# A gated pooling and neighbourhood-attention layer on one core: gate products and operand differences moved to GpSimd, attention's gate taken out of its operand set, heads packed evenly

## The chip, the cores and the metric

One core of a Trainium2 chip runs the whole layer as one program. The metric is the device time of one execution in microseconds (us), the median over the runs shown. Engines are called TensorE (PE in the profile; PEld is its weight load), VectorE (DVE), ScalarE (ACT), GpSimd (POOL) and SyncE (SP). Each works through its own queue in order.

## The reference, cut to what matters

There are 512 + 256 tokens of 2048 features, all in float32.

```python
ada = jax.nn.silu(c) @ w_ada + b_ada
shift, scl, gate = jnp.split(ada, 3, axis=-1)
h = _rms(x, norm_g) * (1 + scl[:, None, :]) + shift[:, None, :]
proj = h @ w_in
...
pool_u, pool_z, q, k, v, attn_z, g_pool, g_attn = jnp.split(proj, cuts, axis=-1)
pool_y = _pool_mixer(pool_u, pool_w, pool_scale) * jax.nn.silu(pool_z)
...
attn_y = _neighbourhood_attention(q, k, v, rpb) * jax.nn.silu(attn_z)
merged = jax.nn.sigmoid(g_pool) * (pool_y @ w_pool_up) + jax.nn.sigmoid(g_attn) * (attn_y @ w_attn_up)
return x + gate[:, None, :] * (merged @ w_o)
```

`proj` has 80 tiles of 128 features: 8 each of pool_u, pool_z, q, k, v and attn_z, 16 of g_pool and 16 of g_attn.

## The kernel before, in words

Activations lie with features on the 128 partitions and all 768 tokens along the free dimension, in tiles of 128x768 float32 (two halves of 384). A "slot" of the `slab` pool holds one such tile; there are 45 (`SLOTS`, L44), and the builder counts what is live.

**Products.** Each float32 number is cut into a high part (a cast to float32r) and a low part (the rest), and a product is three matmuls: high by high, high by low, low by high. A matmul has 128x128 weights and 384 columns. Two output features are made together by `pair_job` (L345), a scheme with seven products (`PRODUCTS`, L47) in place of eight: it needs sums of weights (`add`, L351) and differences of operands. So an operand `Set` (L187) holds, for each of four pairs of feature tiles, four raw quarters (B11, B12, B21, B22) and four differences (T1 to T4), each a slot with a high and a low half. `put` (L191) makes one: ScalarE casts the high part (L194), and VectorE subtracts for the low part (L198), which is held back in `behind` until the next put (`flush`, L181). `differences` (L215) makes T1 to T4 in place, on VectorE (L218, L222, L223, L230), each right before its put. `build` (L237) lists the tasks of a set: load two tiles, optionally work on them (`make`), put four quarters, then four differences. The weights go through `split_next` (L320): cast on ScalarE (L329), subtraction on VectorE (L330), three products ahead of use.

**Stages.** XA and XB are the two halves of `h` (1024 features each) against `w_in`; XA's results are stored as partial sums (`part_d`), XB's are added to them by an accumulating DMA. XR is the pooled branch against `w_pu`, XY the attention branch against `w_au`, MA and MB are the two halves of `merged` against `w_o`. Each of the last four stages (`eight`, L968) has an opening of two features by plain products (16 steps), and seven pair jobs of 14 steps. A step is six matmuls. The opening reads all four pairs' raw quarters within its 16 steps, the differences follow from the 17th step on.

**Order of the work.** The program is written out by a planner. `steps` (L423) yields once a step; `tick` (L168) then runs what was planned for this step (`at`, `after`) and `pump` (L158), which takes the first task of the list if its condition holds, if there is room in the slots (tasks' need plus `heap["spare"]`) and if the pace allows: every third step among pair products, every second where the set is being used up (`drop`), every step among plain products. It also takes `chores`, spaced by their own numbers. If a product needs an operand that is not there, `need` (L284) takes tasks at once until it is (`hurry`). The engines' waits follow from the data.

**Around the change.** XB ends with 32 pair jobs of which eight heads' q, k, v are part. `attention` (L549) plans the six units of a head, 7 or 8 steps apart, by `at`; the first five heads (`DENSE`, L862) begin 42 steps apart, the last three 56, with one or two gate jobs between. When attention's steps have been run (`run(done)`, L1191), XR's set and then XY's are built (L1196, L1197), 31 steps before XB's last step. XY's set loads the attention output and its gate feature (`attended`, L1171), takes Silu of it on ScalarE and multiplies on VectorE (`gated`, L1176): four tiles a pair. The results of XR and XY pass `pu_done` (L904) and `au_done` (L914): a sigmoid of a stored gate tile on ScalarE (`sig_take`, L900) when the result is ready, a product on VectorE, then a store, or an accumulating add and a store. `x_make` (L1135) scales and modulates XB's tiles on VectorE.

```python
def need(st, op, j):
    hurry["on"] = True
    while (op, j) not in st.ops:
        assert tasks and room() >= tasks[0][0] and tasks[0][1](), (st.name, op, j, heap, len(tasks))
        tasks.pop(0)[2]()
```

Of the kernel before, what the change touches and what calls it, by code (L numbers as in the profile page):

```python
# [43 lines left out]
SLOTS = 45  # L44
# [7 lines left out]
def encoder_layer(ctx: ExitStack, tc: tile.TileContext, xT, cT, w_ada2, w_ada4, b_ada, norm_g, w_in, pool_w,  # L52
# [134 lines left out]
    class Set:  # L187
# [3 lines left out]
        def put(self, op, j, src, then=None):  # L191

            t = self.ops[op, j] = slot(f"{self.name}{op}", F32R)
            act.copy(t[:, 0, :], src)  # L194
            flush()

            def rest():
                dve.tensor_tensor(t[:, 1, :], src, t[:, 0, :].bitcast(F32), op=ALU.subtract)  # L198
                if then is not None:
                    then()  # L200

            behind["fn"] = rest
            behind["of"] = t
# [10 lines left out]

    def differences(st, j, a, b):  # L215

        def t1():
            dve.tensor_tensor(a[:, 0, :], a[:, 0, :], a[:, 1, :], op=ALU.subtract)  # L218
            st.put("T1", j, a[:, 0, :])

        def t2():
            dve.tensor_tensor(a[:, 1, :], b[:, 1, :], a[:, 1, :], op=ALU.subtract)  # L222
            dve.scalar_tensor_tensor(b[:, 1, :], a[:, 0, :], -1.0, b[:, 1, :], op0=ALU.mult, op1=ALU.subtract)  # L223
            st.put("T2", j, b[:, 1, :])

        def t3():
            st.put("T3", j, a[:, 1, :], free)

        def t4():
            dve.scalar_tensor_tensor(b[:, 0, :], b[:, 1, :], -1.0, b[:, 0, :], op0=ALU.mult, op1=ALU.subtract)  # L230
            st.put("T4", j, b[:, 0, :], free)

        return t1, t2, t3, t4
# [3 lines left out]
    def build(st, load, ready=lambda j: True, make=None, more=0, whole=0):  # L237


        got = [{} for _ in range(st.pairs)]  # L240

        def fetch(j):
            got[j]["a"], got[j]["b"] = load(j)
            got[j]["t"] = clock["now"]

        def put(j, op):
            k, h = RAW[op]
            st.put(op, j, got[j][k][:, h, :])

        def diff(j, n):  # L250
            g = got[j]
            if n == 0:
                g["d"] = differences(st, j, g["a"], g["b"])
            g["d"][n]()

        def fetches(j):
            tasks.append((2 + more, lambda: ready(j), lambda: fetch(j)))

        def puts(j):
            here = lambda: clock["now"] >= got[j]["t"] + 5 or hurry["on"]  # L260
            if make is not None:
                for k in "ab":
                    tasks.append((0, here, lambda k=k: make(j, k, got[j][k])))
            for op in RAW:
                tasks.append((1, here, lambda op=op: put(j, op)))

        for j in range(whole):
            fetches(j)
            puts(j)
            for n in range(4):  # L270
                tasks.append((1, lambda: True, lambda j=j, n=n: diff(j, n)))
        if whole < st.pairs:
            fetches(whole)
        for j in range(whole, st.pairs):
            if j + 1 < st.pairs:
                fetches(j + 1)
            puts(j)
        for n in range(4):
            for j in range(whole, st.pairs):
                tasks.append((1, lambda: True, lambda j=j, n=n: diff(j, n)))  # L280
# [581 lines left out]
    DENSE = 5  # L862
# [32 lines left out]
    def sig_load(f):  # L895
        state["sig", f] = slot("sig")
        sp.dma_start(flat(state["sig", f]), part_d[G0 + f])

    def sig_take(f):
        t = state["sig", f]  # L900
        act.activation(flat(t), flat(t), AF.Sigmoid)  # L901
        return t

    def pu_done(f):  # L904
        def go(i, t):
            sg = sig_take(f)
            dve.tensor_tensor(flat(t), flat(t), flat(sg), op=ALU.mult)
            pool.dma_start(mp_d[f], flat(t))
            free()
            release(t, 3)  # L910
            sig_load(f + 2)
        return go

    def au_done(f):  # L914
        def go(i, t):
            sg = sig_take(16 + f)
            dve.tensor_tensor(flat(t), flat(t), flat(sg), op=ALU.mult)  # L917
            free()
            if 16 + f + 2 < 32:
                sig_load(16 + f + 2)  # L920

            def add():
                pool.dma_start(flat(t), mp_d[f], accum_op=ALU.add)
                after(5, out)
# [5 lines left out]
            add()  # L930
# [74 lines left out]
    with tc.tile_pool(name="start", bufs=1, reuse_waits="tile") as sp_:  # L1005
# [44 lines left out]
        def modulate(g):  # L1050
# [14 lines left out]
            after(4, rest_)  # L1065
# [69 lines left out]
        def x_make(j, k, t):  # L1135
            dve.tensor_tensor(flat(t), flat(t), flat(rstd), op=ALU.mult)
            apply(8 + 2 * j + (k == "b"), t)
# [33 lines left out]
    def attended(j):  # L1171
        got = stored(attn_d, 2 * j)
        state["az", j] = stored(part_d, AZ0 + 2 * j)
        return got

    def gated(j, k, t):  # L1176
        z = state["az", j][k == "b"]
        act.activation(flat(z), flat(z), AF.Silu)
        dve.tensor_tensor(flat(t), flat(t), flat(z), op=ALU.mult)
        free()  # L1180

    with tc.tile_pool(name="attn", bufs=1, reuse_waits="tile") as at_:
# [7 lines left out]
        done = first - 56 + 40 + 16 - now  # L1190
# [6 lines left out]
    build(XY, attended, lambda j: True, gated, 2, 1)  # L1197
    run(31 * 14 - done)
    for f in range(2):
        sig_load(f)  # L1200
    run(16 + 7 * 14)
# [94 lines left out]
```

## Time and profile before

| | |
|---|---|
| three runs, us | 2041.11, 2044.99, 2046.67 |
| median, us | 2044.99 |
| the profiled execution, us | 2051.03 |
| its span from first to last instruction, us | 2049.3 |
| TensorE busy in the span | 1939.6 us (95%) |
| VectorE, ScalarE, GpSimd busy | 1330.4 us (65%), 1023.1 us (50%), 259.8 us (13%) |
| mean granted TensorE clock, full speed = 1 | 0.973 |

Matmuls are pipelined, so a busy TensorE is not one at its peak; the count of matmuls in a stretch tells more. Idle time of the other engines costs nothing by itself. A wait is put down to what released it last.

### The profile page before, as it was taken

What the parts mean: (1) busy time and instruction counts of PE and PEld (TensorE: products, weight loads), DVE (VectorE), ACT (ScalarE), POOL (GpSimd) and SP (SyncE); (2) the same over time, 40 slices, a digit from 0 to 9 for tenths busy, and PEclk for the clock granted to TensorE, in tenths of its full rate; (3) what the DMA queues carried; (4) which work ended last, traced back from release to release, by engine and by line L of the source; (5) the groups of instructions that cost most, each with busy time, mean ns of one, the idle gap of its engine ahead of it and who ended that gap; (6) DMA issues with size and microseconds to landing.
All of it is one profiled execution on the core that took longest, in us unless ns stands there. A gap on an engine that the chain in (4) does not pass through costs nothing. (4 is left out here: it accounts for less than half of the span.)

```text
span 2049.3 us, 31584 instructions
## 1 busy us (share of the span) xinstructions
PE 1939.6 (95%) x11812; PEld 1832.7 (89%) x11812; DVE 1330.4 (65%) x2392; ACT 1023.1 (50%) x2207; POOL 259.8 (13%) x385
## 2 busy tenths in 40 slices
PE   3999999999999989999999999999989979999998
PEld 2889888898999979999998999999979968999997
DVE  5755555555667777866666667667667767776654
ACT  4433333333344444545656566565556555556553
POOL 0000000000000045410000010010100001112111
PEclk9999999999999999999999999999989989999999
DMA  9755555554343425554544344554556556867765
GB/s 355 248 197 188 190 191 191 201 192 157 117 150 138 162 57 143 135 132 106 119 106 122 93 110 122 109 121 123 132 164 216 214 158 180 243 180 191 211 172 144
DMA packets 100361, 331.92 MB, mean 162 GB/s; under 512 B 13168, under 2 KB 18288, under 8 KB 100208
## 3 DMA queue, kind: packets, MB, share of 16 engines
q1 hardware_dynamic: 68256, 217.35, 31.5%
q0 software_dynamic: 30944, 112.48, 23.8%
q8 instruction: 92, 1.51, 0.3%
q14 instruction: 61, 0.50, 0.1%
q10 hardware_dynamic: 1008, 0.09, 0.0%
HBM read 251.22 MB, written 78.64 MB: 161 GB/s over the span
## 5 line engine op out<-in xcount | busy, mean ns | idle before, releaser
L330 DVE TENSOR_TENSOR wlo<-wraw,whi 128x512 fp32r<-128x512 f32 (+1 forms) x357 | 247.2, 693 | 300.7 <-ACT whi L329 294.8
L330 DVE TENSOR_TENSOR wlo<-wsum,whi 128x512 fp32r<-128x512 f32 x420 | 292.7, 697 | 126.6 <-ACT whi L329 124.5
L440 PE MATMUL acc<-xbT,whi 128*128 128x384 f32 x1248 | 338.4, 352 | 10.6 <-ACT u L368 8.4
L329 ACT CAST whi<-wsum 128x512 fp32r<-128x512 f32 x420 | 260.4, 620 | 150.0 <-ACT whi L329 47.2
L440 PE MATMUL acc<-xaT,whi 128*128 128x384 f32 x1216 | 313.5, 338 | 1.1 <-ACT u L368 0.6
L329 ACT CAST whi<-wraw 128x512 fp32r<-128x512 f32 (+1 forms) x357 | 215.8, 605 | 97.4 <-PE acc L440 71.0
L368 ACT COPY u<-acc 128x384 f32<-128x384 f32 x210 | 100.5, 478 | 299.8 <-PE acc L440 299.8
L440 PE MATMUL acc<-xbB,whi 128*128 128x384 f32 x936 | 245.7, 343 | 0.5 <-DVE o L757 0.5
L440 PEld LDWEIGHTS acc<-xbT,whi 128*128 128x128 f32 x1248 | 226.2, 194 | 19.3 <-ACT u L368 10.6
L440 PE MATMUL acc<-xaB,whi 128*128 128x384 f32 x912 | 235.3, 338 | 0.0
L440 PEld LDWEIGHTS acc<-xaT,whi 128*128 128x128 f32 x1216 | 217.5, 188 | 16.2 <-issue 14.4
L440 PE MATMUL acc<-xbT,wlo 128*128 128x384 f32 x624 | 214.8, 344 | 0.0
L440 PE MATMUL acc<-xaT,wlo 128*128 128x384 f32 x608 | 203.7, 335 | 0.0
L440 PEld LDWEIGHTS acc<-xaB,whi 128*128 128x128 f32 x912 | 163.0, 188 | 11.9 <-issue 9.9
L440 PEld LDWEIGHTS acc<-xbB,whi 128*128 128x128 f32 x936 | 165.7, 189 | 6.0 <-issue 1.4
L440 PE MATMUL acc<-xbB,wlo 128*128 128x384 f32 x468 | 157.2, 336 | 0.0
L353 DVE TENSOR_TENSOR wsum<-wraw 128x512 f32<-128x512 f32 x210 | 145.1, 691 | 13.7 <-DMA wraw<-in_w_in_dram 13.6
L440 PE MATMUL acc<-xaB,wlo 128*128 128x384 f32 x456 | 152.8, 335 | 0.0
L353 DVE TENSOR_TENSOR wsum<-wsum,wraw 128x512 f32<-128x512 f32 x210 | 147.7, 703 | 0.2
L440 PEld LDWEIGHTS acc<-xbT,wlo 128*128 128x128 f32 x624 | 121.1, 194 | 0.0
L382 ACT ACTIVATE o<-acc 128x384 f32<-128x384 f32 x105 | 51.6, 492 | 125.3 <-PE acc L440 125.0
L440 PEld LDWEIGHTS acc<-xaT,wlo 128*128 128x128 f32 x608 | 114.1, 188 | 0.0
(251 smaller groups left out, 3435.4 us busy)
## 6 DMA issues: line engine op xcount, KB each, us to landing
wraw<-in_w_in_dram SPq DMA_DIRECT2D x160, 512.0 KB, 4.3
adaw<-in_w_ada_dram SPq DMA_DIRECT2D x96, 512.0 KB, 5.4
part_d<-o POOLq DMA_DIRECT2D x116, 384.0 KB, 2.9
wraw<-in_w_o_dram SPq DMA_DIRECT2D x32, 512.0 KB, 6.2
o<-part_d POOLq DMA_DIRECT2D x38, 384.0 KB, 4.8
sig<-part_d SPq DMA_DIRECT2D x32, 384.0 KB, 6.2
wraw<-in_w_pu_dram SPq DMA_DIRECT2D x16, 512.0 KB, 4.5
wraw<-in_w_au_dram SPq DMA_DIRECT2D x16, 512.0 KB, 5.0
```

What stands on the lines that cost most here:

```text
L329: act.copy(hi[:, :n, :], raw)
L330: dve.tensor_tensor(lo[:, :n, :], raw, hi[:, :n, :].bitcast(F32), op=ALU.subtract)
L353: dve.tensor_tensor(t[:, :n, :], a, b, op=ALU.add)
L368: act.copy(t, c["a"][:, :TH])
L382: act.activation(c["o2"][:, 0, :], c["a"][:, :TH], AF.Copy, scale=-1.0)
L440: pe.matmul(out, w, m, start=s["first"] and j == 0 and k == 0, stop=j == n - 1 and k == 2, skip_group_check=True)
```

## The change

`SLOTS` becomes 46 and `DENSE` 8. The differences of a pair are made by `combine`, four operations on GpSimd, as one task after the four raw puts; their puts come at least four steps later. With `combine`'s signs T2 is the negative of before, so its cast and its subtraction turn the sign. `build` orders the load of the next pair ahead of a pair's difference puts. The sigmoids are taken six steps after the gate tile's load, and the products with them go to GpSimd. The attention gate is a row of chores during XR (`gated`): for each of eight features it loads the attention output and the gate, multiplies them on GpSimd, takes the sigmoid of the gate, multiplies again and stores; XY's set then loads the stored result, two tiles a pair. In `x_make` the product with rstd goes to GpSimd and the modulation to ScalarE.

```diff
--- before.py
+++ after.py
@@ -41,7 +41,7 @@
 CHUNKS = [(0, 64), (64, 128), (192, 128), (320, 128), (448, 64), (512, 96), (608, 64), (672, 96)]
 SMALL = 64
 
-SLOTS = 45
+SLOTS = 46
 PAIRS = 4
 
 PRODUCTS = (("w11", "B11"), ("s1", "T1"), ("s2", "T2"), ("w12", "B21"), ("s3", "T3"), ("w22", "T4"), ("s4", "B22"))
@@ -191,11 +191,17 @@
         def put(self, op, j, src, then=None):
 
             t = self.ops[op, j] = slot(f"{self.name}{op}", F32R)
-            act.copy(t[:, 0, :], src)
+            if op == "T2":
+                act.activation(t[:, 0, :], src, AF.Copy, scale=-1.0)
+            else:
+                act.copy(t[:, 0, :], src)
             flush()
 
             def rest():
-                dve.tensor_tensor(t[:, 1, :], src, t[:, 0, :].bitcast(F32), op=ALU.subtract)
+                if op == "T2":
+                    dve.scalar_tensor_tensor(t[:, 1, :], src, -1.0, t[:, 0, :].bitcast(F32), op0=ALU.mult, op1=ALU.subtract)
+                else:
+                    dve.tensor_tensor(t[:, 1, :], src, t[:, 0, :].bitcast(F32), op=ALU.subtract)
                 if then is not None:
                     then()
 
@@ -212,25 +218,17 @@
                 del self.ops[op, j]
                 free()
 
+    def combine(a, b):
+
+        pool.tensor_tensor(a[:, 0, :], a[:, 0, :], a[:, 1, :], op=ALU.subtract)
+        pool.tensor_tensor(a[:, 1, :], b[:, 1, :], a[:, 1, :], op=ALU.subtract)
+        pool.tensor_tensor(b[:, 1, :], a[:, 0, :], b[:, 1, :], op=ALU.add)
+        pool.tensor_tensor(b[:, 0, :], b[:, 1, :], b[:, 0, :], op=ALU.subtract)
+
     def differences(st, j, a, b):
 
-        def t1():
-            dve.tensor_tensor(a[:, 0, :], a[:, 0, :], a[:, 1, :], op=ALU.subtract)
-            st.put("T1", j, a[:, 0, :])
-
-        def t2():
-            dve.tensor_tensor(a[:, 1, :], b[:, 1, :], a[:, 1, :], op=ALU.subtract)
-            dve.scalar_tensor_tensor(b[:, 1, :], a[:, 0, :], -1.0, b[:, 1, :], op0=ALU.mult, op1=ALU.subtract)
-            st.put("T2", j, b[:, 1, :])
-
-        def t3():
-            st.put("T3", j, a[:, 1, :], free)
-
-        def t4():
-            dve.scalar_tensor_tensor(b[:, 0, :], b[:, 1, :], -1.0, b[:, 0, :], op0=ALU.mult, op1=ALU.subtract)
-            st.put("T4", j, b[:, 0, :], free)
-
-        return t1, t2, t3, t4
+        return (lambda: st.put("T1", j, a[:, 0, :]), lambda: st.put("T2", j, b[:, 1, :]),
+                lambda: st.put("T3", j, a[:, 1, :], free), lambda: st.put("T4", j, b[:, 0, :], free))
 
     RAW = {"B11": ("a", 0), "B12": ("a", 1), "B21": ("b", 0), "B22": ("b", 1)}
 
@@ -247,29 +245,37 @@
             k, h = RAW[op]
             st.put(op, j, got[j][k][:, h, :])
 
-        def diff(j, n):
-            g = got[j]
-            if n == 0:
-                g["d"] = differences(st, j, g["a"], g["b"])
-            g["d"][n]()
+        def mix_(j):
+            flush()
+            combine(got[j]["a"], got[j]["b"])
+            got[j]["d"] = differences(st, j, got[j]["a"], got[j]["b"])
+            got[j]["t"] = clock["now"]
+
+        def since(j, n):
+            return lambda: clock["now"] >= got[j]["t"] + n or hurry["on"]
 
         def fetches(j):
             tasks.append((2 + more, lambda: ready(j), lambda: fetch(j)))
 
         def puts(j):
-            here = lambda: clock["now"] >= got[j]["t"] + 5 or hurry["on"]
             if make is not None:
                 for k in "ab":
-                    tasks.append((0, here, lambda k=k: make(j, k, got[j][k])))
+                    tasks.append((0, since(j, 5), lambda k=k: make(j, k, got[j][k])))
             for op in RAW:
-                tasks.append((1, here, lambda op=op: put(j, op)))
-
+                tasks.append((1, since(j, 8 if make is not None else 5), lambda op=op: put(j, op)))
+            tasks.append((0, lambda: True, lambda: mix_(j)))
+
+        def diffs(j, ns=range(4)):
+            for n in ns:
+                tasks.append((1, since(j, 4), lambda n=n: got[j]["d"][n]()))
+
+        fetches(0)
         for j in range(whole):
-            fetches(j)
             puts(j)
-            for n in range(4):
-                tasks.append((1, lambda: True, lambda j=j, n=n: diff(j, n)))
-        if whole < st.pairs:
+            if j + 1 < whole:
+                fetches(j + 1)
+            diffs(j)
+        if 0 < whole < st.pairs:
             fetches(whole)
         for j in range(whole, st.pairs):
             if j + 1 < st.pairs:
@@ -277,7 +283,7 @@
             puts(j)
         for n in range(4):
             for j in range(whole, st.pairs):
-                tasks.append((1, lambda: True, lambda j=j, n=n: diff(j, n)))
+                diffs(j, (n,))
 
     hurry = {"on": False}
 
@@ -859,7 +865,7 @@
 
     jobB = lambda a, b, da, db, last=False: pair_job(XB, cut(w_in, a, 1), cut(w_in, b, 1), both(da, db), last)
     GR = (3, 2, 1, 0)
-    DENSE = 5
+    DENSE = 8
 
     def pool_up(g):
         for i in range(2):
@@ -893,41 +899,33 @@
 
 
     def sig_load(f):
-        state["sig", f] = slot("sig")
-        sp.dma_start(flat(state["sig", f]), part_d[G0 + f])
-
-    def sig_take(f):
-        t = state["sig", f]
-        act.activation(flat(t), flat(t), AF.Sigmoid)
-        return t
+        t = state["sig", f] = slot("sig")
+        sp.dma_start(flat(t), part_d[G0 + f])
+        after(6, lambda: act.activation(flat(t), flat(t), AF.Sigmoid))
+
+    def gate_with(f, t):
+        pool.tensor_tensor(flat(t), flat(t), flat(state["sig", f]), op=ALU.mult)
+        free()
+        if f + 2 < 32:
+            sig_load(f + 2)
 
     def pu_done(f):
         def go(i, t):
-            sg = sig_take(f)
-            dve.tensor_tensor(flat(t), flat(t), flat(sg), op=ALU.mult)
+            gate_with(f, t)
             pool.dma_start(mp_d[f], flat(t))
-            free()
-            release(t, 3)
-            sig_load(f + 2)
+            release(t, 4)
         return go
 
     def au_done(f):
         def go(i, t):
-            sg = sig_take(16 + f)
-            dve.tensor_tensor(flat(t), flat(t), flat(sg), op=ALU.mult)
-            free()
-            if 16 + f + 2 < 32:
-                sig_load(16 + f + 2)
-
-            def add():
-                pool.dma_start(flat(t), mp_d[f], accum_op=ALU.add)
-                after(5, out)
+            gate_with(16 + f, t)
+            pool.dma_start(flat(t), mp_d[f], accum_op=ALU.add)
 
             def out():
                 pool.dma_start(merged_d[f], flat(t))
                 state.setdefault("merged", set()).add(f)
                 release(t, 3)
-            add()
+            after(6, out)
         return go
 
     SPANS = ((0, NS, 0), (NS, T, 1))
@@ -1062,7 +1060,8 @@
                 for fn in differences(XA, j, a, b):
                     fn()
 
-            after(4, rest_)
+            after(3, lambda: (flush(), combine(a, b)))
+            after(7, rest_)
 
         SKIP = 2
 
@@ -1133,8 +1132,11 @@
             return got
 
         def x_make(j, k, t):
-            dve.tensor_tensor(flat(t), flat(t), flat(rstd), op=ALU.mult)
-            apply(8 + 2 * j + (k == "b"), t)
+            kt = 8 + 2 * j + (k == "b")
+            pool.tensor_tensor(flat(t), flat(t), flat(rstd), op=ALU.mult)
+            for s, (a, b) in enumerate(((0, NS), (NS, T))):
+                act.activation(flat(t)[:, a:b], flat(t)[:, a:b], AF.Identity, scale=scale[:, kt, s : s + 1],
+                               bias=shift[:, kt, s : s + 1])
 
         modulated = 6 + 5 * KT * 4 + 8 * 4 + 6
         run(modulated)
@@ -1169,15 +1171,39 @@
         return got
 
     def attended(j):
-        got = stored(attn_d, 2 * j)
-        state["az", j] = stored(part_d, AZ0 + 2 * j)
-        return got
-
-    def gated(j, k, t):
-        z = state["az", j][k == "b"]
-        act.activation(flat(z), flat(z), AF.Silu)
-        dve.tensor_tensor(flat(t), flat(t), flat(z), op=ALU.mult)
-        free()
+        return stored(attn_d, 2 * j)
+
+    def gated():
+
+        t = [[slot("ga"), slot("gz")] for _ in range(2)]
+
+        def load(f):
+            sp.dma_start(flat(t[f % 2][0]), attn_d[f])
+            sp.dma_start(flat(t[f % 2][1]), part_d[AZ0 + f])
+
+        def first(f):
+            o, z = (flat(q) for q in t[f % 2])
+            pool.tensor_tensor(o, o, z, op=ALU.mult)
+
+        def second(f):
+            o, z = (flat(q) for q in t[f % 2])
+            act.activation(z, z, AF.Sigmoid)
+
+        def third(f):
+            o, z = (flat(q) for q in t[f % 2])
+            pool.tensor_tensor(o, o, z, op=ALU.mult)
+            pool.dma_start(attn_d[f], o)
+            state.setdefault("gated", set()).add(f)
+
+        load(0)
+        load(1)
+        for f in range(8):
+            chores.append((2, lambda f=f: first(f)))
+            chores.append((2, lambda f=f: second(f)))
+            chores.append((3, lambda f=f: third(f)))
+            if f + 2 < 8:
+                chores.append((0, lambda f=f: load(f + 2)))
+        chores.append((0, lambda: free(4)))
 
     with tc.tile_pool(name="attn", bufs=1, reuse_waits="tile") as at_:
         state["pool"] = at_
@@ -1187,18 +1213,20 @@
         for p in range(8):
             attention(p, first, 7 if p < DENSE else 8)
             first += 42 if p < DENSE else 56
-        done = first - 56 + 40 + 16 - now
+        done = first + 9 - now
         run(done)
 
 
     outs["pool"] = ctx.enter_context(tc.tile_pool(name="outs", bufs=1, reuse_waits="tile"))
     heap["spare"] = 1
     build(XR, pooled, whole=2)
-    build(XY, attended, lambda j: True, gated, 2, 1)
-    run(31 * 14 - done)
+    run((len(jobs) - 1) * 14 - done)
     for f in range(2):
         sig_load(f)
-    run(16 + 7 * 14)
+    run(16)
+    gated()
+    build(XY, attended, lambda j: {2 * j, 2 * j + 1} <= state.get("gated", set()), whole=2)
+    run(7 * 14)
     build(MA, lambda j: stored(merged_d, 2 * j), lambda j: {2 * j, 2 * j + 1} <= state.get("merged", set()), whole=2)
     build(MB, lambda j: stored(merged_d, 8 + 2 * j), lambda j: {8 + 2 * j, 9 + 2 * j} <= state.get("merged", set()), whole=2)
     run(3 * (16 + 7 * 14))
```

## Rows read from the trace of the kernel before

**Rows 1.** XB, XR, XY, MA: length; PE, PEld, DVE, ACT, POOL busy (xcount); PEclk, DMA, GB/s.

```profile
705.50:1499.90 794.40, 771.64 (x4654) 729.21 (x4653) 543.81 (x1045) 446.85 (x1123) 137.66 (x183) 0.97 0.49 117
1499.90:1643.00 143.10, 129.59 (x686) 126.13 (x686) 102.35 (x172) 84.71 (x146) 8.46 (x15) 0.93 0.55 194
1643.00:1792.80 149.80, 129.79 (x685) 124.84 (x684) 107.63 (x179) 78.40 (x145) 21.57 (x30) 0.93 0.70 198
1792.80:1917.90 125.10, 121.10 (x687) 120.09 (x686) 87.68 (x155) 75.63 (x151) 23.43 (x32) 0.99 0.75 197
```

**Rows 2.** The same view of shorter stretches.

```profile
1830.00:1910.00 80.00, 80.00 (x462) 79.63 (x461) 54.99 (x96) 49.72 (x98) 16.44 (x22) 1.00 0.76 190
...
1500.00:1560.00 60.00, 50.05 (x249) 47.84 (x248) 41.62 (x73) 35.07 (x63) 3.07 (x5) 0.89 0.51 171
...
1643.00:1710.00 67.00, 51.23 (x237) 47.23 (x236) 43.98 (x74) 34.06 (x62) 6.68 (x10) 0.85 0.50 148
...
700.00:790.00 90.00, 76.36 (x402) 73.04 (x402) 67.78 (x104) 38.72 (x78) 37.12 (x48) 0.93 0.43 109
...
750.00:860.00 110.00, 104.82 (x586) 102.93 (x586) 84.92 (x129) 56.35 (x109) 56.26 (x81) 0.98 0.50 119
```

**Rows 3.** TensorE's waits, 1470 to 2050 us: total, times, longest.

```profile
PE acc L440 <- ACT p L368: 15.8, 4, 6.8
...
PE acc L440 <- ACT u L368: 10.8, 10, 2.1
```

**Rows 4.** ScalarE by line, 1500 to 1710: xcount, busy, mean ns, idle before, releasers.

```profile
L194 ACT CAST xyT<-in 128x384 fp32r<-128x384 f32 x16 | 8.2, 512 | 18.8 <-DVE in L223 7.2 <-DVE in L218 6.2 <-DVE in L230 5.4
...
L901 ACT ACT_TABLE_LOAD x6 | 7.7, 1283 | 0.1
...
L1178 ACT ACT_TABLE_LOAD x5 | 6.4, 1283 | 0.1
```

**Rows 5.** SyncE's queue in order of time, 1495 to 1660: start, us, what.

```profile
1502.35 2.25 SPq L1167 DMA_DIRECT2D in<-pooled_d  x4
...
1645.86 0.93 SPq L1167 DMA_DIRECT2D in<-attn_d  x2
```

**Rows 6.** VectorE by line, 1500 to 1643 us.

```profile
L330 DVE TENSOR_TENSOR wlo<-wsum,whi 128x512 fp32r<-128x512 f32 x28 | 19.2, 686 | 4.7 <-ACT whi L329 4.5
...
L907 DVE TENSOR_TENSOR o<-o,sig 128x768 f32<-128x768 f32 x12 | 11.5, 959 | 11.0 <-ACT sig L901 10.5
...
L375 DVE TENSOR_TENSOR o<-acc,p 128x384 f32<-128x384 f32 x7 | 3.9, 553 | 1.0 <-PE acc L440 1.0
...
L218 DVE TENSOR_TENSOR in<-in 128x384 f32<-128x384 f32 x4 | 2.2, 550 | 0.0
```

**Rows 7.** GpSimd by line and shape, whole span.

```profile
L712 POOL TENSOR_TENSOR sum<-u 128x799 f32<-128x799 f32 x8 | 13.2, 1648 | 13.7 <-ACT u L704 13.7
...
L927 POOL DMA_DIRECT2D merged_d<-o x14 | 8.2, 586 | 33.9 <-DMA o<-mp_d 29.1 <-issue 4.8
...
L908 POOL DMA_DIRECT2D mp_d<-o x14 | 7.6, 540 | 107.3 <-DVE o L907 107.3
```

**Rows 8.** VectorE in order of time, 758 to 763: start, us, what.

```profile
760.62 1.99 DVE L330 TENSOR_TENSOR wlo<-wraw,whi 128x512 fp32r<-128x512 f32 x1
...
762.54 0.54 DVE L375 TENSOR_TENSOR o<-acc,p 128x384 f32<-128x384 f32 x1
```

**Rows 9.** GpSimd in order of time, 756 to 765.

```profile
758.31 6.05 POOL L712 TENSOR_TENSOR sum<-sum 128x797 f32<-128x797 f32 x3
```

**Rows 10.** GpSimd's stores of heads 4 to 7, in order of time.

```profile
1183.82 0.57 POOL L672 DMA_DIRECT2D attn_d<-o  x1 [1.41 <-ACT o L670]
...
1248.82 0.57 POOL L672 DMA_DIRECT2D attn_d<-o  x1 [1.41 <-ACT o L670]
...
1315.12 0.58 POOL L672 DMA_DIRECT2D attn_d<-o  x1 [12.70 <-ACT o L670]
...
1393.10 0.58 POOL L672 DMA_DIRECT2D attn_d<-o  x1 [12.69 <-ACT o L670]
```

## The prediction, made before the changed kernel was run

> **What bounds the kernel now.** I read the page first, then the busy times cut at the first matmul of each stage, then TensorE's waits inside the worst stretches, and last what ScalarE, VectorE and the queues do there. TensorE works all through the span; what can be won is where it stands still or runs at the lower clock.
>
> A stretch without a stall has 462 matmuls in 80 us, 0.1732 us each [rows 2]. One of the last four stages is 114 steps of six matmuls, 684 in all: 118.5 us at that pace. Measured are 143.1 us for the pool up-projection (XR), 149.8 for the attention up-projection (XY) and 125.1 for the first half of the output projection (MA) [rows 1]: 24.6, 31.3 and 6.6 us are lost. Most of it lies at the openings: 1500 to 1560 holds 249 matmuls, 43.1 us of work in 60; 1643 to 1710 holds 237, 41.0 in 67 [rows 2]. The opening of XB is of the same kind: 700 to 790 holds 402, 69.6 in 90, with VectorE busy 67.8 of them [rows 2].
>
> TensorE's longest waits there name ScalarE's copies out of PSUM (p and u) [rows 3]. ScalarE is not busy in them: it stands in front of casts of T operands until VectorE has made the difference that the cast reads, 18.8 us before the 16 xyT casts alone [rows 4], and everything behind that cast waits, the copies and the weights' high parts too. So difference, cast and low part go back and forth between two queues that work in order. They are made that late because the loads are late: XR's last four tiles are issued at 1502.35, after the opening has begun at 1499.9, and XY's last pair at 1645.86, after 1643.0 [rows 1, 5].
>
> **The change, part by part.**
>
> Packing the heads. Eight heads of 42 steps take 336 instead of 378; with the shorter allowance behind the last head, attention's run is 370 steps instead of 403. The steps of XB are fixed, so 64 are left for XR's operands before its opening, not 31. A pair costs some ten tasks, one in three steps: two pairs fit into 64, one into 31. The price: heads 42 steps apart store their output 65.0 us apart, heads 56 apart 78.0 us [rows 10]. A step is six matmuls, 1.04 us, which leaves 65.0 - 43.7 = 21.3 us and 78.0 - 58.2 = 19.8 us beside the products. 1.5 us more for each of the three heads that become denser is 4.5 us lost; between 0 (only the same work sooner) and three times that if the last heads fare worse, I take 4.5.
>
> XR's opening. With pairs 0 and 1 made before it and the loads of 2 and 3 issued about when it begins, ten steps before their use, the forced making at the opening ends. Of the 24.6 us lost in the stage, 16.9 lie in that first stretch. A set that was made on the planner's pace is MA: it still loses 6.6 us in its stage. The remainder for a well-prepared set is between 0 and 6.6; I take 4, as MA's own wait was the same back and forth and the differences now come from another queue.
>
> XY's opening. The gate leaves the set. Its eight feature tiles are loaded, multiplied and stored during XR, so a pair needs two tiles and not four, and one more slot is there. By the slots, pair 0 is made while the gate still holds four, pair 1 after they come free, some 35 steps ahead of the opening, and pairs 2 and 3 are loaded in XR's last job, whose finished operands free slots. The stage loses 31.3 us, 26.0 of them in its first stretch; again I leave 4. The Silu passes go, and with them their changes of ScalarE's table: 11 loads of 1.28 us in 1500 to 1710 become one [rows 4]. These 12.8 us are ScalarE's and stand in the openings already counted; nothing is added. The gate's store is read again by SP, so SP may stand a few us before a load, with weight loads queued behind it: between 0 and 5 us for each of two pairs, taken inside the contention term below.
>
> Gate products on GpSimd. 14 of 0.96 us leave VectorE in XR's stage (12 in the row [rows 6], two of the opening's), and their sigmoids are taken six steps after the load, so ScalarE no longer makes VectorE wait. On GpSimd a product of 128x799 takes 1.65 us [rows 7]; 768 columns by the same rate are 1.58 us. Each delays its output's store by that, and nothing reads the store soon.
>
> Differences on GpSimd. Four of 0.55 us a pair leave VectorE [rows 6]; on GpSimd half of 1.58, 0.79 us, or 3.2 us a pair, started four steps (4.2 us) before the first cast. So a cast meets a finished difference as long as GpSimd's queue is less than about a us behind. T2 with its sign turned keeps the kinds and sizes of its copy and subtraction: nothing.
>
> XB's operands. The multiplication by rstd goes to GpSimd, the modulation to ScalarE. VectorE, 75% busy in 700 to 790, loses 8 x 0.96 for the products and 16 x 0.55 for the differences, 16.5 us besides the modulation. 20.4 us are lost there; a gain of none up to all. I take 8, since the pooling mixer's own waits and a late weight load stand in the same stretch. The start (XA) has the same moved differences, but its T operands are used a dozen steps later: nothing, 3 us either way.
>
> **What GpSimd takes back.** During XR it gets 16 gate-tile products for attention, some 15 gate products and 16 half-width differences: 31 x 1.58 + 16 x 0.79 = 61.6 us, and with 16 stores of 0.54 us [rows 7] and eight more of the gate about 75 us of 131. A row shows what that does: while three GpSimd additions ran for 6.05 us [rows 9], VectorE's subtractions with both inputs in SBUF took up to 1.99 us, against 0.69 ordinarily, and one with an input in PSUM took its usual 0.54 [rows 6, 8]. The nearest stretch is 750 to 860, where GpSimd was busy 56.3 of 110 us: 586 matmuls are 101.5 us, so 8.5 us were lost [rows 2]. In XR I take 8, in XY (half that GpSimd work) 5, in MA 0.5; at least nothing, at most the third rival.
>
> **Sum.** XR 118.5 + 4 + 8 = 130.5 for 143.1: -12.6. XY 118.5 + 4 + 5 = 127.5 for 149.8: -22.3. MA 125.1 to 122: -3. XB -8 + 4.5 = -3.5. Together -41.4 us. The profiled execution took 2051.0 us, its span 2049.3; that gives 2009.6. The median of the runs shown, 2045.0, lies 6.0 us below the profiled one: 2003.6, called 2004.
>
> **The rivals.**
>
> *More is won.* GpSimd's work costs TensorE nothing, and the openings are clean: -24.6 - 31.3 - 6.6 and half of XB's 20.4 make -73, 1972 us. For it: the denser GpSimd stretch lost part of its 8.5 us to other things. Chance 0.12 for under 1985.
>
> *The shared port.* Every GpSimd operation holds back one VectorE operation with two SBUF inputs by 1.3 us (1.99 - 0.69), half that for a half-width one: 31 x 1.3 + 16 x 0.65 = 51 us in XR. VectorE's 102.4 us there [rows 1], less 13.4 for gate products, 3.8 for four attention products of the same size and 8.8 for 16 differences, become 76 + 51 = 127 us of work in one queue, over the stage's 118.5; with the unevenness of such work XR stays at about 143 and XY at 133: -3 - 3.5 - 17 = -23, about 2022 us. It decides once GpSimd is at work for more than half of a stage. The Trainium skill, GPSIMD Engine Reference, sections 1 (Specifications) and 8 (Key points), says that GpSimd shares its SBUF interfaces with VectorE and contends with VectorE instructions that have two SBUF inputs. The trace agrees, by the 1.99 against 0.54 us above. Chance 0.15.
>
> *The change does not do what it says.* The slots don't suffice, XY's first two pairs are again not ready, and its stage stays at 149.8 us: -41.4 + 22.3 = -19, 2026 us. Against it: two tiles fewer a pair. Chance 0.08.
>
> *Slower: GpSimd's queue.* Each pair's first T cast waits at the head of ScalarE's queue for a difference that stands behind other GpSimd work: a gate product that waits for its output, a store of merged that waits for its accumulating transfer (29.1 us of such waits before 14 stores [rows 7], 2.1 each). The 16 later pairs of XB, XR, XY and MA, and four of MB, lose the head start of 4.2 us and the rest stands before TensorE. From 41.4 / 20 = 2.1 us a pair on, the change loses; at 4 us it costs 80 and gives 2045 - 41 + 80 - 3 (for the waits already in it), about 2081. Against it: GpSimd is idle over 40% of the fullest stage. Chance 0.10.
>
> **How the numbers follow.** The forecast as told, 1985 to 2018, has 0.50; more won 0.12; the port 0.15; the slots 0.08; slower 0.10; and 0.05 for a result within 0.3% (6 us, about what a measurement here can tell from no change), where gains and prices happen to meet. Faster: 0.50 + 0.12 + 0.15 + 0.08 = 0.85. The range leaves out the slower case and the far end of the large gain and takes in both smaller gains: 1976 to 2038.
>
> **What would show it.** The stages at about 130, 127 and 122 us between their first plain matmuls; no ScalarE wait on differences, at most a us before a T cast; one table load in XR and XY; XR's last loads before its opening and XY's in XR's last job; GpSimd busy over half of XR, with VectorE's splits there at 0.8 to 0.9 us. I would be wrong if ScalarE's T casts wait on GpSimd, if SP's loads of attn_d hold back weights, or if the last three heads stall TensorE.

## The result, and the profile after

The changed kernel takes 2058.36 us (median of 4 runs, 2054.37 to 2059.16) against 2044.65 before: a ratio of 1.0065, 95% interval [1.0046, 1.0084]. It is slower; 2004 was forecast, with 2038 as the range's upper end and a chance of 0.10 for slower.

The stages of the kernel after, cut at their first plain matmuls as in [rows 1] (XB, XR, XY, MA, and MB with the end; columns: stretch, length, busy us of PE, PEld, DVE, ACT, POOL, PEclk, DMA share, GB/s):

```profile
707.40:1514.40 807.00, 775.53 (x4654) 729.91 (x4653) 541.82 (x1031) 448.30 (x1131) 159.09 (x201) 0.97 0.49 116
1514.40:1670.00 155.60, 131.46 (x687) 124.34 (x686) 128.46 (x135) 76.50 (x143) 94.00 (x70) 0.93 0.62 217
1670.00:1795.90 125.90, 121.67 (x686) 119.91 (x684) 108.99 (x134) 67.95 (x130) 73.98 (x62) 0.99 0.80 226
1795.90:1921.30 125.40, 121.25 (x686) 119.97 (x685) 93.58 (x138) 76.20 (x154) 47.00 (x50) 0.99 0.78 209
1921.30:2057.20 135.90, 121.81 (x686) 120.01 (x685) 74.48 (x118) 63.96 (x125) 33.27 (x42) 0.97 0.59 151
```

XY fell from 149.8 to 125.9 us, 1.6 better than forecast. XR rose from 143.1 to 155.6 where 130.5 was forecast, XB from 794.4 to 807.0 where 790.9 was, and MB with the end (the last stage) from 131.4 to 135.9. In XR VectorE does fewer instructions (135 for 172 in [rows 1]) in more time (128.5 us for 102.4).

VectorE by line in XR. First the kernel before, 1500 to 1643 us (its other split, of summed weights, took 0.69 us [rows 6]), then the kernel after, 1515 to 1640 us:

```profile
L330 DVE TENSOR_TENSOR wlo<-wraw,whi 128x512 fp32r<-128x512 f32 x24 | 16.5, 686 | 3.0 <-ACT whi L329 3.0
```

```profile
L336 DVE TENSOR_TENSOR wlo<-wraw,whi 128x512 fp32r<-128x512 f32 x17 | 27.4, 1613 | 5.7 <-ACT whi L335 5.7
L336 DVE TENSOR_TENSOR wlo<-wsum,whi 128x512 fp32r<-128x512 f32 x22 | 22.5, 1025 | 10.3 <-ACT whi L335 10.1
```

The same splits that took 0.69 us take 1.0 to 1.6 us in the mean, while VectorE's output operations with one input in PSUM stay at 0.54 to 0.55 us. And ScalarE stands before things that another queue has not delivered. ScalarE's waits over the whole span (total us, times, longest):

```profile
ACT gz L1190 <- POOL ga L1186: 20.4, 5, 10.1
...
ACT xb L1138 <- POOL xb L1136: 14.1, 4, 9.4
...
ACT sig L904 <- DMA sig<-part_d: 12.2, 8, 4.5
...
ACT mbT L197 <- POOL in L223: 7.0, 1, 7.0
```

In the opening of XB it looks like this, GpSimd first, then ScalarE, both in order of time (start, us, what):

```profile
714.89 0.77 POOL L1157 MEMSET u<- 128x800 f32 x1 [3.18 <-DMA part_d<-o]
715.63 1.01 POOL L223 TENSOR_TENSOR xb<-xb 128x384 f32<-128x384 f32 x1
...
718.88 0.99 POOL L226 TENSOR_TENSOR xb<-xb 128x384 f32<-128x384 f32 x1
719.83 3.56 POOL L1136 TENSOR_TENSOR xb<-xb,rstd 128x768 f32<-128x768 f32 x2
```

```profile
721.66 1.30 ACT L1138 ACTIVATE xb<-xb,shift,scale 128x512 f32<-128x512 f32 x2 [9.42 <-POOL xb L1136]
```

The last pair's product stands behind a memset that waited for the memory of stored outputs, and behind four differences; ScalarE waits 9.4 us for it, and TensorE 7.3 us for the cast behind that. What the change was to take away is gone, though: no cast of a T operand of XY waits any more (18.8 us in [rows 4]). ScalarE by line, 1514 to 1796 us:

```profile
L197 ACT CAST xyT<-in 128x384 fp32r<-128x384 f32 x12 | 6.1, 509 | 0.0
...
L904 ACT ACT_TABLE_LOAD x1 | 1.3, 1283 | 0.0
```

### The profile page after: what moved, and what is told of

It reads as the page before. It is cut to its first block, busy times and chain, and to the rows that moved or that the text cites. A ratio compares the mean times of both kernels' runs of the same rounds, so it can differ in the third digit from the quotient of the medians.

```text
span 2057.2 us, 31762 instructions
## 1 busy us (share of the span) xinstructions
PE 1938.9 (94%) x11812; PEld 1826.9 (89%) x11812; DVE 1365.6 (66%) x2232; ACT 1014.0 (49%) x2213; POOL 490.7 (24%) x545
## 4 chain that ended last, share of the span: by engine, by line
PE 51%; issue 5%; DVE 5%; ACT 3%; POOL 3%; DMA 3%; SPq 0%; POOLq 0%; DVEq 0%; ACTq 0%
PE acc L446 43%; PE op L668 2%; DVE wlo L336 2%; PE acc L464 1%; DVE wsum L359 1%; PE n L509 1%; PE s L574 1%; PE pt L635 1%; DMA sig<-part_d 1%; DMA wraw<-in_w_in_dram 1%; ACT whi L335 1%; PE yk L545 1%; POOL o L907 1%; DMA merged_d<-o 0%; DVE xyB L204 0%
## 5 line engine op out<-in xcount | busy, mean ns | idle before, releaser
L336 DVE TENSOR_TENSOR wlo<-wraw,whi 128x512 fp32r<-128x512 f32 (+1 forms) x357 | 289.2, 811 | 301.1 <-ACT whi L335 296.9
L336 DVE TENSOR_TENSOR wlo<-wsum,whi 128x512 fp32r<-128x512 f32 x420 | 318.2, 758 | 128.5 <-ACT whi L335 125.9
L446 PEld LDWEIGHTS acc<-xaT,whi 128*128 128x128 f32 x1216 | 217.5, 188 | 19.2 <-issue 14.4
L776 POOL DMA_DIRECT2D part_d<-o x76 | 41.2, 542 | 540.1 <-ACT o L388 471.5
L359 DVE TENSOR_TENSOR wsum<-wsum,wraw 128x512 f32<-128x512 f32 x210 | 167.5, 798 | 0.3
L359 DVE TENSOR_TENSOR wsum<-wraw 128x512 f32<-128x512 f32 x210 | 157.0, 748 | 14.5 <-DMA wraw<-in_w_in_dram 14.5
L782 POOL DMA_DIRECT2D part_d<-o x40 | 34.7, 867 | 389.3 <-ACT o L388 179.2
```

The costliest lines, as they stand in the source:

```text
L336: dve.tensor_tensor(lo[:, :n, :], raw, hi[:, :n, :].bitcast(F32), op=ALU.subtract)
L359: dve.tensor_tensor(t[:, :n, :], a, b, op=ALU.add)
L446: pe.matmul(out, w, m, start=s["first"] and j == 0 and k == 0, stop=j == n - 1 and k == 2, skip_group_check=True)
L776: pool.dma_start(part_d[f], flat(t))
L782: pool.dma_start(part_d[f], flat(t), accum_op=ALU.add)
```

## The experiments

Two theories stood at first. **Queue**: moved work makes ScalarE, SyncE or GpSimd stand at the head of a queue that works in order, with TensorE's operands behind it. **Port**: GpSimd's operations slow VectorE's, which then sets the pace. Times are medians, and ratios are to the kernel before on the same chip (its medians there lie between 2042.7 and 2045.2 us). Stage times come from the one profiled execution of each kernel, which is not always near the median: e4's took 2041.9 us, e7's 2052.4. XB varies by up to 8 us between executions of the same code (790.8 to 798.8 in e5 and e8 to e11, whose XB is the same; 794.4 before, 788.1 in e6, where XB is untouched), the last four stages by up to 3 (MA 125.1 before and 122.1 in e6), XR and XY by 0.1 there.

| kernel | us | ratio [95%] | XB | XR | XY | MA | MB, end |
|---|---|---|---|---|---|---|---|
| changed | 2058.4 | 1.0065 [1.0046, 1.0084] | 807.0 | 155.6 | 125.9 | 125.4 | 135.9 |
| e1 | 2049.4 | 1.0030 [1.0018, 1.0043] | 796.4 | 155.7 | 126.0 | 124.0 | 136.3 |
| e2 | 2058.4 | 1.0083 [1.0061, 1.0105] | 805.1 | 153.3 | 128.5 | 126.9 | 135.1 |
| e3 | 2049.8 | 1.0026 [1.0011, 1.0040] | 802.6 | 153.1 | 128.5 | 127.0 | 135.9 |
| e4 | 2033.6 | 0.9947 [0.9929, 0.9966] | 803.2 | 153.0 | 121.9 | 122.5 | 130.4 |
| e5 | 2016.4 | 0.9864 [0.9845, 0.9883] | 795.5 | 141.2 | 120.2 | 121.9 | 130.4 |
| e6 | 2071.1 | one run | 788.1 | 143.1 | 149.9 | 122.1 | 160.3 |
| e7 | 2058.0 | 1.0061 [1.0039, 1.0082] | 798.2 | 163.1 | 125.7 | 123.7 | 134.1 |
| e8 | 2023.5 | 0.9884 [0.9858, 0.9911] | 798.7 | 144.6 | 120.6 | 122.4 | 130.4 |
| e9 | 2004.7 | 0.9798 [0.9771, 0.9824] | 798.8 | 129.0 | 120.3 | 121.4 | 130.3 |
| e10 | 2003.5 | 0.9800 [0.9782, 0.9817] | 796.9 | 129.2 | 120.3 | 120.5 | 130.4 |
| e11 | 2029.1 | 0.9918 [0.9894, 0.9941] | 790.8 | 152.3 | 121.3 | 122.1 | 130.4 |
| e12 | 2052.0 | 1.0044 [1.0022, 1.0066] | 805.2 | 148.8 | 126.3 | 126.2 | 135.9 |

**e1: XB's product back on VectorE.**

```diff
-            pool.tensor_tensor(flat(t), flat(t), flat(rstd), op=ALU.mult)
+            dve.tensor_tensor(flat(t), flat(t), flat(rstd), op=ALU.mult)
```

> XB's product with rstd is back on VectorE, all else as changed. Queue theory (ScalarE stands at the head of its queue before something GpSimd has not made yet): the 14.1 us of ScalarE's wait for that product go, the opening of XB loses some 8 us less, 2050 us in all; the other stages stay as they are. Port theory (GpSimd's operations slow VectorE's by the shared port): nearly nothing changes, since VectorE was idle for 12 us in that stretch; VectorE even has 8 x 0.96 us more to do: 2056 to 2062. Packing theory (the denser heads cost it): no change.

9 us less (7 by the ratios). ScalarE now waits for VectorE's product instead, 12.5 us in all and so nearly as long, but in seven pieces of at most 2.5 us; the one of 9.4 us is gone, and TensorE's 7.3 us behind it with it. The queue theory holds for this place.

**e2: the attention gate's sigmoid in a slot of its own.**

```diff
-            act.activation(z, z, AF.Sigmoid)
+            act.activation(g, z, AF.Sigmoid)
...
-            pool.tensor_tensor(o, o, z, op=ALU.mult)
+            pool.tensor_tensor(o, o, g, op=ALU.mult)
```

> The attention gate's sigmoid is written to a slot of its own, so ScalarE no longer waits until GpSimd has read the gate; GpSimd's work and its order are the same. Queue theory: the 20.4 us of ScalarE's wait go and XR's stage falls from 155.6 to 140 to 148 us, 2045 to 2050 in all. Port theory: GpSimd is as busy as before beside VectorE, XR stays at 153 to 157.

All 20.4 us of ScalarE's waits on the gate went, XR gave 2.3 us and XY took 2.6. For this place the queue theory's price falls. Other waits took over in XR: ScalarE stood 29.3 us for VectorE's weight sums, as before (29.0), and its waits for gate tiles that had not landed grew from 5.9 to 10.8 us. The edit also takes two more slots, and in XY a T cast now waits (3.5 us).

**e3: both edits.**

> Both edits. Queue theory: the two add, 2036 to 2043 us, level with the kernel before or below it. Port theory: over 2052.

2049.8, no better than e1 alone. The two edits don't add; what is left must be elsewhere.

**e4: the differences on VectorE.**

```diff
-        pool.tensor_tensor(a[:, 0, :], a[:, 0, :], a[:, 1, :], op=ALU.subtract)
+        dve.tensor_tensor(a[:, 0, :], a[:, 0, :], a[:, 1, :], op=ALU.subtract)
...
```

(and the other three of `combine`)

> The four differences of a pair are made on VectorE, at the same place in the program; the rest as changed. Queue theory: the cast that waited 7.0 us in MB no longer waits, MB's stage falls by 4 us; XB's product no longer stands behind four differences, so XB loses some 4 us less; XR loses a few us less as well, since GpSimd's queue is shorter: 2040 to 2052. Port theory: VectorE has 8.8 us more a set and GpSimd 18 us less beside it, 2050 to 2058. If the differences on GpSimd are a gain in themselves: over 2062.

2033.6, better than both theories had it, and faster than the kernel before. XY, MA and MB fall by 4.0, 2.9 and 5.5 us, XR by only 2.6. In MB it is the forecast's slower rival at one place. GpSimd and ScalarE of the changed kernel there:

```profile
1936.29 0.56 POOL L942 DMA_DIRECT2D half_d<-o  x1 [7.27 <-DMA o<-in_xT_dram]
1936.86 1.04 POOL L223 TENSOR_TENSOR in<-in 128x384 f32<-128x384 f32 x1
```

```profile
1937.93 0.51 ACT L197 CAST mbT<-in 128x384 fp32r<-128x384 f32 x1 [7.02 <-POOL in L223]
```

A store waits for its accumulating transfer, the difference waits behind it, the cast waits for the difference. This run takes away both what the differences cost VectorE and such waits; it doesn't tell the two apart.

**e5: all that was moved to GpSimd back on VectorE**, at the changed places (e1, e4, the product in `gate_with`, the two products in `gated`).

> Everything that the change moved to GpSimd is on VectorE again (XB's products, the differences, the gate products, attention's two products a feature), at the changed places in the program: what is left is the order, the packing, the early sigmoids and the stored gate. Port theory: with GpSimd idle beside it VectorE's operations take their ordinary time, XR falls from 153 to 130 to 140 us although VectorE has more to do, XY stays at 122 to 128, 2010 to 2028 in all. If VectorE's own load is the bound (some 115 us of work in XR, in one queue): XR stays over 148, 2035 or more.

2016.4, 42 us less than the changed kernel, and 28 less than before. What is left of the change (order, packing, stored gate, 46 slots, the modulation on ScalarE) is a gain together, nearly all of it in XY, 120.2 us for 149.8; the work on GpSimd took it back. XR is still 141.2.

**e6: GpSimd's work alone.** The kernel before, with products that nobody reads, in MB.

```diff
+    def more():
+        a, b = (flat(q) for q in extra["t"])
+        pool.tensor_tensor(a, a, b, op=ALU.mult)
+
+    after(20, begin)
+    after(22, lambda: chores.extend((3, more) for _ in range(26)))
```

> The kernel before, with 26 GpSimd products of 128x768 added in MB's stage, one every third step, on two slots that nobody else reads: nobody waits for them, their result is dropped. Port theory: VectorE's operations with two SBUF inputs grow beside them, mean of the splits over 0.9 us in that stage, VectorE's 74.8 us become about 105, and TensorE loses 3 to 12 us, as VectorE has no slack in its dependent chains. Queue theory: nobody waits for GpSimd, so TensorE loses nothing but what late output transfers cost at the end, under 2 us.

MB with the end goes from 131.4 to 160.3 us, far past the port theory's 12. The kernel before: the stretch and VectorE's splits of raw weights (1930 to 2040; those of summed weights took 0.69 us too).

```profile
1917.90:2049.30 131.40, 119.67 (x686) 118.39 (x684) 74.77 (x127) 64.91 (x127) 24.48 (x34) 0.98 0.63 163
```

```profile
L330 DVE TENSOR_TENSOR wlo<-wraw,whi 128x512 fp32r<-128x512 f32 x20 | 13.8, 689 | 16.6 <-ACT whi L329 16.6
```

With the edit: the stretch, the splits (1930 to 2050) and the added line.

```profile
1908.80:2069.10 160.30, 130.55 (x687) 124.10 (x685) 121.60 (x127) 64.50 (x127) 77.54 (x62) 0.94 0.51 134
```

```profile
L330 DVE TENSOR_TENSOR wlo<-wraw,whi 128x512 fp32r<-128x512 f32 x19 | 31.9, 1678 | 9.7 <-ACT whi L329 9.7
L330 DVE TENSOR_TENSOR wlo<-wsum,whi 128x512 fp32r<-128x512 f32 x25 | 30.8, 1234 | 11.2 <-ACT whi L329 10.4
```

```profile
L1214 POOL TENSOR_TENSOR ea<-ea,eb 128x768 f32<-128x768 f32 x26 | 54.5, 2096 | 0.9
```

28.9 us for 26 products, 1.1 us each, with nobody waiting for them. All of it lies among the matmuls: the last one begins 9.5 us before the end in both kernels (2039.75 and 2059.59), so late output transfers have no part in it. 10.9 us are TensorE's own busy time, at a granted clock of 0.94 for 0.98; the rest is waiting. VectorE has the same 127 instructions, and 121.6 us of work for 74.8. It is busy 76% of the stage, and 89.2 of the 104 us in which the products run: it need not be full to hold TensorE up. TensorE's weight loads wait 8.0 us for splits and 6.8 for one of VectorE's output operations, and for neither in the kernel before.

**e7: heads packed as before.**

```diff
-    DENSE = 8
+    DENSE = 5
```

> DENSE is 5 again, the rest as changed: the last three heads are 56 steps apart, and 22 steps instead of 64 are left for XR's operands. Forecast's theory: the packing costs 4.5 us in XB and wins XR's prepared opening; without it XB is 4 us shorter and XR's stage longer by some 8 us than 155.6; 2058 to 2066 in all. If the packing is a net loss: under 2054.

Level in all. XR is 7.5 us longer, as its operands are late again (four tiles are issued at 1506.0 us, after the opening at 1504.0). XB is 8.8 shorter in the profiled execution, hardly more than XB varies by.

**e8: only attention's two products a feature on GpSimd.**

> XB's products, the differences and the gate products are on VectorE; only attention's two products a feature stay on GpSimd. Port theory: 16 GpSimd products in the first 60 us of XR hold back some 16 VectorE operations by 1.3 us each, 20 us on a queue that is full there: XR 5 to 10 us longer than with all on VectorE. Queue theory: ScalarE's sigmoid waits for GpSimd's first product, whose queue is short now: no wait over 2 us. If VectorE's load is the bound, this one is faster than with all on VectorE, by 3 to 8 us in XR.

XR is 3.4 us longer than in e5; the intervals of the two ratios overlap. The 3.4 us are a balance: VectorE is busy 12.1 us longer in XR with 17 instructions fewer, while ScalarE's waits for gate tiles that had not landed fell from 18.7 to 5.6 us. The longest wait of attention's sigmoid is 3.4 us, not under 2.

**e9: as e5, the sigmoids later.**

```diff
-        after(6, lambda: act.activation(flat(t), flat(t), AF.Sigmoid))
+        after(11, lambda: act.activation(flat(t), flat(t), AF.Sigmoid))
```

> All on VectorE as in the earlier run, and the sigmoids of the gate tiles are taken 11 steps after their load instead of 6. Theory: what is left in XR's 141.2 us is ScalarE standing at the head of its queue before sigmoids whose tile has not landed (18.7 us in six waits, the longest 7.7, with a stop of TensorE of the same length behind it): XR falls by 5 to 9 us, 2007 to 2013 in all. Rival: VectorE, 112 us busy of the 141, sets XR: under 2 us change.

XR falls by 12.2 us, more than expected. In e5 ScalarE stood 20.6 us in all before sigmoids whose tile had not landed; in e9 no such wait is left. XR in e5 and in e9:

```profile
1499.80:1641.00 141.20, 126.54 (x687) 123.54 (x686) 111.86 (x182) 77.07 (x143) 12.84 (x23) 0.95 0.71 246
```

```profile
1503.60:1632.60 129.00, 122.02 (x685) 119.79 (x684) 111.05 (x180) 76.34 (x143) 12.84 (x23) 0.99 0.76 266
```

Nearly the same work on every engine, 12 us apart. 4.5 of the 12.2 us are TensorE's own busy time, at a granted clock of 0.95 against 0.99; the rest is waiting. At 2004.7 us this kernel beats the one before and the changed one.

**e10: and the stored tile read back later.**

```diff
-            state.setdefault("gated", set()).add(f)
+            after(7, lambda: state.setdefault("gated", set()).add(f))
```

> The same, and a gated tile counts as stored seven steps after its store was issued, so that the load of XY's set does not make SyncE stand (8.7 us) before the store has landed, with weight and gate loads behind it. Theory (queues that work in order): that wait falls under 2 us, XR by another 0 to 4 us, XY unchanged within 2 us. Rival (the loads are early enough anyway): no change to the run with late sigmoids, within 2 us.

No change. SyncE's wait before XY's set is gone, but it stands longer before the gate's own loads (40.5 us for 32.1), and XR is level (129.2 for 129.0).

**e11: XB's products and the differences on VectorE.**

> XB's products and the differences on VectorE, the gate products and attention's two products on GpSimd as changed. It stands between the run with the differences alone on VectorE (2033.6) and the one that also has the gate products there (2023.5). If the prices add: 2033.6 - 9 = 2024.6, and the gate products cost next to nothing on GpSimd. If the port's price goes by GpSimd's work alone: 32 gate products fewer beside VectorE are worth over 15 us, so this one is 2030 to 2038.

2029.1, between the two. Beside e8, where the gate products are on VectorE too, XR is 7.7 us longer and XY 0.7. So 16 gate products in XY cost next to nothing and 15 in XR, where GpSimd has attention's products as well, about half a us each. The intervals of the two ratios overlap.

**e12: the changed kernel with late sigmoids** (e9's edit alone).

> The changed kernel with one edit: its sigmoids 11 steps after the load, all GpSimd work as changed. If the waits of the early sigmoids cost XR as much here as with all on VectorE (12 us): XR 144 to 148, 2044 to 2050 in all. If the port is the bound of XR here, with VectorE full from 1590 on, the sigmoids' waits are hidden behind it: XR 152 to 157, 2052 to 2060.

XR falls by 6.8 us, the whole to 2052.0, in the middle (its interval overlaps the changed kernel's). ScalarE's waits for gate tiles that had not landed go from 12.2 us to 0.3 over the whole span. In XR they were 5.9 us here and 18.7 in e5: there was less to win, and nothing shows that any of it was hidden.

## Why the prediction was wrong

**Stalls and their cause: right, as far as the runs tell.** The forecast had the openings lose their time to the exchange of differences and casts between two queues, and to late loads. With XY's set loaded early the stage fell by 23.9 us for 22.3 forecast; no T cast waits in it, and one table load is left of eleven. With the differences back on VectorE (e5) XY is even 120.2 us: it was their place in the order that helped, not the engine. The early loads, the stored gate and the early differences were not run apart.

**Packing: right, and a little small.** From the first head's store to XB's end take 516.1 us, before 512.2: 3.9 us more, 4.5 forecast. Over all runs it is 508.4 to 512.2 us in the three kernels with `DENSE` 5 and 512.2 to 520.6 in the eleven with 8, 6 us apart in the mean. The other 8.7 us of XB lie before that store.

**What GpSimd takes back: the step that failed.** It was put at 8 us in XR, 5 in XY, 0.5 in MA and nothing in MB. Four kernels that differ by two edits alone give its price: the moved work on GpSimd or on VectorE, with the sigmoids 6 steps after the load (changed, e5) or 11 (e12, e9). On GpSimd it costs 42 us with the early sigmoids and 47 with the late ones. By stages that is 14.4 and 19.8 us in XR, 5.7 and 6.0 in XY, 3.5 and 4.8 in MA, 5.5 and 5.6 in MB; XB's 11.5 and 6.4 are uncertain by XB's own 8. So XY was right, XR got about half of its price, and MA, MB and XB were missed.

The rows had the pieces: a split at 1.99 us beside a GpSimd addition [rows 8, 9], and 8.5 us lost in 750 to 860. But XR's 8 us were taken over from that stretch by GpSimd's busy share, 51% there and 57% forecast for XR, as if every busy us were alike. The stretch has 15 additions of 785 to 799 columns, 26.7 of GpSimd's 56.3 us; the rest is eight-column operations and DMA issues. XR has 31 wide products and 16 differences of half the width, 81 of 94.0 us. Laid on the wide operations alone, the 8.5 us are 0.57 each, which makes an estimate of 22 us for XR, near the 19.8. But one price does not carry from stage to stage: counted the same way it is 0.25 us in XY and 1.1 in e6. What sets it was not found.

The shared port, a rival with 0.15, had the load right: 127 us of VectorE work in XR, 128.5 measured. It put the stage at about 143; measured are 155.6, and 148.8 without the early sigmoids (e12). Splits that arrive late stop TensorE before VectorE is full, as e6 shows. The rival's condition, GpSimd at work for over half of a stage, held in XY too (74.0 of 125.9 us), which came out 1.6 us under the forecast, not at 133.

The Trainium skill, GPSIMD Engine Reference, section 8 (Key points), has the contention with two SBUF inputs as a rule; the trace agrees, with splits at 1.0 to 1.6 us for 0.69 and operations with a PSUM input unchanged at 0.54, and adds what it costs here. The same page's section 4.1 (Engine selection) advises VectorE for elementwise work, GpSimd being about twice as slow with two inputs: 1.84 us for a product of 768 columns against 0.96, which agrees; that GpSimd was idle made it look free.

**The early sigmoids: a wait that was not looked for.** "ScalarE no longer makes VectorE wait" was costed at nothing. But the sigmoid itself now stood at the head of ScalarE's queue before a transfer that landed late, with the weights' casts behind it: 11.7 us from e5 to e9, 6.3 in the changed kernel (e12). The prediction has no term for what is queued behind a moved instruction.

**XB's products: wrong sign.** A gain of 8 was taken. ScalarE's modulation stood 9.4 us behind a product in GpSimd's queue; e1 gives 9 us back. XB's first part, up to the first head's store, is 284.5 to 290.9 us in the five kernels with this product on GpSimd and 278.6 to 283.6 in the seven with it on VectorE. Nor is the gain there with all on VectorE: XB is 790.8 to 798.8 in e5 and e8 to e11, against 788.1 and 794.4 untouched.

**The slower rival: the kind, not the size.** Its mechanism, ScalarE before something behind other work in GpSimd's queue, showed at XB's product, at the gate (no gain without it, e2) and before T casts: 7.0 us once in MB, 4.4 in three casts of MA. The 20 pairs with 4 us each did not come; T casts waited for GpSimd 14 us in all. Put those and e1's 9 us to the queue, and some 19 of the 42 us remain without a wait of ScalarE on GpSimd that was shown to cost. That these are the port's is an argument by elimination, beside e6.

**The rest of the sum was near.** Without the 13.5 us of contention and the 8 won in XB it is -46.9 us; e9, with all on VectorE and the sigmoids late, is 40 us under its kernel before. XY is 120.3 us there for 118.5 + 4. XR is 129.0, so its remainder over 118.5 is 10.5 us and not 4: TensorE's weight loads still wait 4.4 us for low parts of XR's T operands, 3.1 for a weight split and 1.7 for copies. Of the 25.1 us that the changed kernel's XR lies over its 130.5, 11.8 are GpSimd's beyond the 8, 6.8 the sigmoids and 6.5 this remainder. Why XB's opening gained nothing stays open.

## What to carry to other kernels

An idle engine that slows a busy one when it works is not free room. Count the wide operations put there and not its busy time, look for a stretch of the trace that shows their price, and try the placement with work that nobody reads: here a wide product cost from next to nothing (XY in e11) to 1.1 us (e6). An instruction moved ahead of its need is a wait at the head of its queue if its input comes by DMA; place it by when the input lands in a late case, not in the usual one. A change that bundles an order with a placement should be run with each alone: here the order and what came with it were worth 28 us (e5; 40 with the sigmoids later, e9), and the placement cost 42. And a wait that the profile names may be worth nothing: 20.4 us of them went in e2, and the time stayed.

## What the runs showed that was not expected

26 GpSimd products of 128x768 that nobody reads made a stage of 131.4 us 28.9 us longer, with VectorE busy 76% of it. Single VectorE operations with two SBUF inputs took up to 2.84 us in the changed kernel's XR, four times their 0.68. A GpSimd product of 768 columns in place took 1.84 us where the addition of 799 columns took 1.65: the estimate of 1.58 from columns alone was 14% short.
